# A two-layer encoder trunk on one core: one plain round of the first feed-forward matrix instead of two, the sums of x formed first, and the last step of the inverse variance moved back

## The chip, the core and the metric

The kernel runs on one core of a Trainium2 chip. The core has TensorE (PE in the profile, with its weight loads as PEld), VectorE (DVE), ScalarE (ACT), GpSimd (POOL), and SyncE (SP), whose queue issues most of the transfers. The metric is device time in microseconds (us) of one run: the median of three runs before is 1065.5 us (1065.3 to 1065.88).

## The reference

Two layers act on 512 rows of width 1024. The mixing part of a layer (three kinds of attention side by side) is not touched by the change. What is touched is the second half of each layer:

```
    x = x + jnp.concatenate([ya, yb, yc], axis=-1) @ w_out
    u = _rms(x, norm2) @ w_ff1
    return x + jnp.square(jax.nn.relu(u)) @ w_ff2
```

Here `_rms` divides a row by the root of its mean square (plus 1e-6) and multiplies it by the gain `norm2`. `w_ff1` is 1024 x 4096 and `w_ff2` is 4096 x 1024. Since relu followed by a square is homogeneous of degree two, the kernel leaves the division out of the first product and multiplies the result of the second by the inverse of the mean square.

## The kernel before

**Precision.** Every float32 matrix product is made of three: each operand is split into a rounded high part and a remainder (`whi`, `wlo` for weights, halves of `xhl` for x), and `mm3` (L262) issues high times high (L263), high times low (L264) and low times high (L265). The split of a weight block of 128x1024 (a "job") is one ScalarE copy (L205, writes `whi`) and one VectorE subtraction (L206, writes `wlo`). There are three buffers for each of `whi` and `wlo`, so a job's split can start once TensorE is done with the job three places earlier.

**The first feed-forward matrix** is worked through in 8 rounds (`NR`), each of 512 of its 4096 columns. The first `NSTD` = 2 rounds are plain: `ff1_std` (L1214) uses 4 jobs of 48 matmuls of 256 columns. The other six use Winograd's form of Strassen's product, which multiplies 2x2 blocks with 7 products instead of 8: `ff1_st` (L1245) uses 7 jobs of 24 matmuls, in the order `ORDER` (A11, S1, S2, A12, S4, S3, A22). S1 and S3 are sums of two blocks of weights that are added as the second is transferred (a second transfer with add, L160, on the GpSimd queue); S2 and S4 are formed by VectorE (L216, L220). A round of this kind also needs sums of blocks of x. `xsums` (L350) forms and splits them, a quarter at each of its 8 steps, in the buffer `xt`, and leaves them in `xbx`. The results of a round are rectified, squared, combined and split by `act`, `csplit`, `n1_`, `n2_`, `tail_` and `gsplit` (L1172 to L1206), mostly on VectorE.

**The second matrix** is worked through in 4 slices (`ff2`, L1306), each of which needs two rounds of the first. A slice has 14 products of 24 matmuls. `ff_pairs` (L117) interleaves one product of the second matrix with one of a Winograd round of the first, after the first `LEAD` = 0 products of the first matrix; both kinds of job stand in one list, and loads and splits run ahead in the order of that list.

**The inverse mean square.** `sqacc` (L322) sums the squares of x: 8 squares on ScalarE (into two halves of the buffer `ms`) and 7 additions on VectorE (L330, into `accs`). `emit_r2` (L1121) multiplies by a matrix of ones (L1123), negates (L1125), takes logarithm and exponential on ScalarE (L1128, L1129) and makes one Newton step on VectorE (L1130, L1131). Its first result (`nv`) is needed by the first `acc` (L1284) of the second matrix, its last (`r2`) only by the last slice. Before, this stood in the first plain round and `xsums` followed it.

**What sets the order.** The program is written as one stream; a scheduler then orders the instructions of each engine, and each engine takes them strictly in that order, waiting on semaphores. PSUM has 8 banks, which `bank()` hands out in turn. A product of `ff1_st` that starts from a copied bank (`Y`, L1248) adds onto it with matmuls that do not clear it.

Of the kernel before, what the change touches and what calls it, by code (L numbers as in the profile page):

```python
# [21 lines left out]
S = 512  # L22
# [22 lines left out]
NS = NR // 2  # L45
NSTD = 2
ORDER = ("A11", "S1", "S2", "A12", "S4", "S3", "A22")
# [3 lines left out]
def trunk(ctx, tc, x, cols, rows, gate_w, tabs, w_in, w_out, w1, w2, out):  # L51
# [43 lines left out]
    def v3(a, d=HD):  # L95
        return a.rearrange("p (h d) -> p h d", d=d)
# [3 lines left out]

    LEAD = 0
    RS_AT = 3
# [49 lines left out]
    free_raw, free_ff = deque(rawt), deque()  # L152
# [298 lines left out]
    for l in range(L):  # L451
# [663 lines left out]

        def bank():
            return banks.popleft()

        rr_ = {}

        def emit_r2():  # L1121
            pv = bank()
            T.matmul(pv, ones_m, sq_acc["t"], start=True, stop=True)  # L1123
            nv, lnv = ms_[:, :S], ms_[:, S:]
            V.tensor_scalar(nv, pv, -1.0, -EPS, ALU.mult, ALU.add)  # L1125
            banks.append(pv)
            r2 = cst.tile([P, S], F32, tag="aux", name=f"r2{l}")
            A.activation(lnv, nv, AF.Ln, scale=-1.0)  # L1128
            A.activation(r2, lnv, AF.Exp, scale=-1.0)  # L1129
            V.tensor_tensor(lnv, nv, r2, ALU.mult)  # L1130
            V.scalar_tensor_tensor(r2, lnv, 2.0, r2, ALU.add, ALU.mult)  # L1131
            rr_.update(nv=nv, r2=r2)

# [80 lines left out]
        def ff1_std(s, rr):  # L1214
            for i in range(2):
# [3 lines left out]
                for j in range(2):  # L1219
# [10 lines left out]
                    if j == 1:  # L1230
# [7 lines left out]
                        else:  # L1238
                            if rr:
                                units.extend(quads)  # L1240
# [4 lines left out]
        def ff1_st(s, rr):  # L1245
            X, Y = bank(), bank()
            prod1(X, 0)
# [58 lines left out]
        def ff2(s):  # L1306
# [37 lines left out]
            for dg in range(2):  # L1344
# [9 lines left out]
                give(s, dg, "t")  # L1354
                if s == 0 and dg:
                    free_ff.append(ms_)
                yield
# [3 lines left out]
        bg = None  # L1361
        for n_ in range(4 * NSTD):
            next(gens[1])
            if n_ == 0:
                for kx in range(KT):
                    sqacc(kx, kx == 0)
            if n_ == 3:
                emit_r2()
            if n_ == 1:
                xt_ = wt("xt", "xt")  # L1370
                bg = xsums(l, *(v3(xt_[:, i * S:(i + 1) * S], 256) for i in range(2)))
            if bg is not None:
                next(bg, None)
                next(bg, None)
        free_ff.append(xt_)
        for which, u in ff_pairs():
            next(gens[which])
        close_phase()
# [60 lines left out]
```

## Time and profile before

| | |
|---|---|
| median of the runs | 1065.5 us (1065.3 to 1065.88) |
| the profiled execution | 1065.74 us, of which the span of the profile is 1064.0 us |
| TensorE busy in the span | 1053.7 us (99%), 8768 matmuls |
| weight loads busy | 1002.8 us (94%) |
| VectorE busy | 904.2 us (85%) |
| ScalarE busy | 627.4 us (59%) |
| feed-forward part of layer 0 | first matmul at 222.78 us |
| feed-forward part of layer 1 | first matmul at 748.25 us |

How to read it: an engine's row gives its busy time, its share of the span and its instructions. Rows of a timeline give the start, the duration, the engine, the line, the operation with output and inputs, the shape, and in brackets how long the engine was idle before it and what it waited for. Instructions overlap at their ends: the pitch from one start to the next is what an instruction costs its engine. A matmul of 256 columns is shown as 0.28 us, but the next one starts 0.11 us later.

### The profile page before, as it was taken

Reading aid. Unit: us, or ns where it says so; the run is one execution under the profiler, and the core shown is the slowest. Engines: PE = TensorE matmul, PEld = TensorE weight load, DVE = VectorE, ACT = ScalarE, POOL = GpSimd, SP = SyncE. Lnnn points to the kernel's source line nnn. Section 1 sums busy time; section 2 is a strip of 40 time slices with the busy share of each in tenths; the row PEclk is TensorE's granted clock in tenths of the full one; section 3 lists DMA queues with packets and bytes.
Section 4 is the critical chain, followed back from the end, with each engine's and each line's share of the span. In section 5 each row is a group of like instructions: output and inputs, shape, how many; then the busy total and the mean of one; then the engine's idle time right before and its main releaser. Section 6 shows DMA issues by size and latency. Waiting matters only on the chain.

```text
span 1064.0 us, 21687 instructions
## 1 busy us (share of the span) xinstructions
PE 1053.7 (99%) x8768; PEld 1002.8 (94%) x8768; DVE 904.2 (85%) x1540; ACT 627.4 (59%) x1097; POOL 102.3 (10%) x154
## 2 busy tenths in 40 slices
PE   8999999999999999999999999999999999999998
PEld 8999977899999999999999998778999999999998
DVE  7696877899997988988977878688999888898797
ACT  6446655376666666567455467444766666666662
POOL 2030020100010000010002200101000101001000
PEclk9999999999999999999999999999999999999999
DMA  6523121165388687676135221213544886767752
GB/s 215 166 98 110 61 68 51 61 193 144 120 211 224 161 217 199 179 215 181 51 110 164 94 80 41 85 46 134 145 120 140 221 215 173 222 181 190 212 134 80
DMA packets 47365, 151.86 MB, mean 143 GB/s; under 512 B 5648, under 2 KB 8848, under 8 KB 47264
## 3 DMA queue, kind: packets, MB, share of 16 engines
q1 hardware_dynamic: 39056, 120.84, 34.0%
q0 software_dynamic: 8064, 29.36, 15.9%
q8 instruction: 69, 1.13, 0.4%
q14 instruction: 32, 0.26, 0.1%
q10 hardware_dynamic: 144, 0.26, 0.1%
HBM read 147.86 MB, written 2.13 MB: 141 GB/s over the span
## 4 chain that ended last, share of the span: by engine, by line
PE 85%; DVE 9%; ACT 3%; issue 1%; DMA 0%; SPq 0%; DVEq 0%
PE at L263 26%; PE at L265 26%; PE at L264 26%; DVE rt L726 2%; DVE wlo L206 2%; PE at L856 1%; PE at L898 1%; PE at L881 1%; ACT pe L769 1%; PE at L979 1%; DVE z L722 1%; DVE z L728 1%; PE at L756 1%; DMA raw<-in_w_in_dram 0%; DVE rb L407 0%
## 5 line engine op out<-in xcount | busy, mean ns | idle before, releaser
L205 ACT ACTIVATE whi<-raw 128x1024 fp32r<-128x1024 f32 (+1 forms) x130 | 136.2, 1048 | 114.6 <-PE at L264 87.8
L264 PE MATMUL at<-xhl,whi 128*128 128x256 f32 (+1 forms) x704 | 198.0, 281 | 0.0
L263 PE MATMUL at<-xhl,whi 128*128 128x256 f32 (+1 forms) x640 | 181.4, 283 | 0.0
L265 PE MATMUL at<-xhl,wlo 128*128 128x256 f32 (+1 forms) x640 | 180.4, 282 | 0.0
L263 PE MATMUL at<-yg,whi 128*128 128x256 f32 (+1 forms) x592 | 179.9, 307 | 0.5 <-DVE xT L1294 0.5
L206 DVE TENSOR_TENSOR wlo<-raw,whi 128x1024 fp32r<-128x1024 f32 (+1 forms) x130 | 157.4, 1211 | 27.0 <-ACT whi L205 26.6
L265 PE MATMUL at<-yg,wlo 128*128 128x256 f32 (+1 forms) x592 | 178.4, 301 | 0.0
L264 PE MATMUL at<-yg,whi 128*128 128x256 f32 (+1 forms) x560 | 169.4, 303 | 0.0
L263 PE MATMUL at<-whi,xhl 128*128 128x256 f32 (+1 forms) x576 | 163.0, 283 | 0.8 <-ACT xhl L334 0.7
L265 PE MATMUL at<-whi,xhl 128*128 128x256 f32 (+1 forms) x576 | 160.5, 279 | 0.6 <-DVE xhl L335 0.6
L264 PE MATMUL at<-wlo,xhl 128*128 128x256 f32 (+1 forms) x576 | 160.3, 278 | 0.5 <-DVE wlo L206 0.5
L205 ACT ACTIVATE whi<-fraw 128x1024 fp32r<-128x1024 f32 x100 | 106.1, 1061 | 83.9 <-PE at L264 79.6
L206 DVE TENSOR_TENSOR wlo<-fraw,whi 128x1024 fp32r<-128x1024 f32 x100 | 122.2, 1222 | 26.2 <-ACT whi L205 25.6
L264 PEld LDWEIGHTS at<-xhl,whi 128*128 128x128 f32 x704 | 132.2, 188 | 1.8 <-issue 0.5
L263 PEld LDWEIGHTS at<-xhl,whi 128*128 128x128 f32 x640 | 120.1, 188 | 1.7 <-ACT ct L1232 0.5
L265 PEld LDWEIGHTS at<-xhl,wlo 128*128 128x128 f32 x640 | 120.1, 188 | 1.2
L263 PEld LDWEIGHTS at<-yg,whi 128*128 128x128 f32 x592 | 111.2, 188 | 6.3 <-issue 1.7
L265 PEld LDWEIGHTS at<-yg,wlo 128*128 128x128 f32 x592 | 111.1, 188 | 5.3
L263 PEld LDWEIGHTS at<-whi,xhl 128*128 128x128 f32 x576 | 108.2, 188 | 1.8 <-ACT xhl L334 0.9
L264 PEld LDWEIGHTS at<-yg,whi 128*128 128x128 f32 x560 | 105.2, 188 | 4.2 <-DVE yg L1009 0.5
L265 PEld LDWEIGHTS at<-whi,xhl 128*128 128x128 f32 x576 | 108.2, 188 | 1.1 <-DVE xhl L335 1.0
L264 PEld LDWEIGHTS at<-wlo,xhl 128*128 128x128 f32 x576 | 108.4, 188 | 0.7 <-DVE wlo L206 0.7
(301 smaller groups left out, 2517.0 us busy)
## 6 DMA issues: line engine op xcount, KB each, us to landing
fraw<-in_w_dram SPq DMA_DIRECT2D x72, 512.0 KB, 4.9
raw<-in_w_dram SPq DMA_DIRECT2D x56, 512.0 KB, 4.3
raw<-in_w_in_dram SPq DMA_DIRECT2D x34, 512.0 KB, 3.5
fraw<-in_w_dram POOLq DMA_DIRECT2D x32, 512.0 KB, 6.3
raw<-in_w_out_dram SPq DMA_DIRECT2D x16, 512.0 KB, 3.2
xt<-in_w_dram SPq DMA_DIRECT2D x16, 512.0 KB, 5.1
raw<-in_w_dram POOLq DMA_DIRECT2D x14, 512.0 KB, 7.2
ms<-in_w_dram SPq DMA_DIRECT2D x12, 512.0 KB, 4.2
```

The source lines that it names most:

```text
L205: A.activation(hi[:, cs_], raw[:, cs_], AF.Copy)
L206: V.tensor_tensor(lo[:, cs_], raw[:, cs_], hi[:, cs_], ALU.subtract)
L263: T.matmul(o, sh, mh, start=first, stop=False, skip_group_check=skip)
L264: T.matmul(o, sh, ml, start=False, stop=False, skip_group_check=skip)
L265: T.matmul(o, sl, mh, start=False, stop=last, skip_group_check=skip)
L722: V.tensor_tensor(z10, z10, bc(rq), ALU.mult)
L726: V.tensor_tensor(r10[:, oo:oo + n, a:a + 32], z10[:, oo:oo + n, b:b + 32], tb(S_, n, a, a + 32), ALU.mult)
L728: V.tensor_tensor(zaq[t], ro[:, :640], rt[:, :640], ALU.add)
L756: T.matmul(sc[r][:, g * 256:g * 256 + nk], qTA[g][r * 64:(r + 1) * 64, c * P:(c + 1) * P], kTA[r * 64:(r + 1) * 64, k0:k0 + nk], start=Tru ...
L769: A.activation(pe[:, u, :nk], sc[u % 2][:, (u // 2) * 256:(u // 2) * 256 + nk], AF.Exp, bias=nmx[:, u:u + 1], accum_out=ssum[:, u:u + 1])
L856: T.matmul(sp[:, :nk], qTB[rs, pr, n * P:(n + 1) * P], kTB[rs, pr, :nk], start=True, stop=False)
L881: T.transpose(pt[:, b * P:(b + 1) * P], scs[r][:, b * P:(b + 1) * P], ident)
```

## The change

`NSTD` becomes 1: round 1 of the first matrix is now a Winograd round. `LEAD` becomes 7: the 7 products of that round come before the first product of the second matrix, and from there on the interleaving is the same as before. `xsums` is now run by the first four steps (two quarters after each plain product), ahead of `sqacc`, which follows after the fifth; `emit_r2` follows after the eighth, and its last two VectorE instructions become `finish_r2`, which is called at the end of the first slice of the second matrix. The buffer `xt` goes back to the ring of load buffers after the fifth step. `bank()` remembers which banks have been used, and `Y` is now taken from those. Lines from L1116 on have other numbers in the changed kernel: L1123, L1125, L1130 and L1131 become L1128, L1130, L1139 and L1140; L1184, L1196, L1199, L1200, L1205, L1264, L1270 and L1293 become those numbers plus 8.

```
-NSTD = 2
+NSTD = 1
...
-    LEAD = 0
+    LEAD = 7
...
-        def bank():
-            return banks.popleft()
+        full = set()
+
+        def bank(seeded=False):
+            b = next(b for b in banks if not seeded or id(b) in full)
+            banks.remove(b)
+            full.add(id(b))
+            return b
...
             A.activation(r2, lnv, AF.Exp, scale=-1.0)
+            rr_.update(nv=nv, lnv=lnv, r2=r2)
+
+        def finish_r2():
+            nv, lnv, r2 = (rr_[n] for n in ("nv", "lnv", "r2"))
             V.tensor_tensor(lnv, nv, r2, ALU.mult)
             V.scalar_tensor_tensor(r2, lnv, 2.0, r2, ALU.add, ALU.mult)
-            rr_.update(nv=nv, r2=r2)
...
-                            if rr:
+                            if rr == NSTD - 1:
                                 units.extend(quads)
...
-            X, Y = bank(), bank()
+            X, Y = bank(), bank(True)
...
                 if s == 0 and dg:
+                    finish_r2()
                     free_ff.append(ms_)
...
-        for n_ in range(4 * NSTD):
-            next(gens[1])
+        for n_, (which, u) in enumerate([(1, None)] * 4 * NSTD + list(ff_pairs())):
+            next(gens[which])
             if n_ == 0:
+                xt_ = wt("xt", "xt")
+                bg = xsums(l, *(v3(xt_[:, i * S:(i + 1) * S], 256) for i in range(2)))
+            if n_ < 4:
+                next(bg)
+                next(bg)
+            if n_ == 4:
                 for kx in range(KT):
                     sqacc(kx, kx == 0)
-            if n_ == 3:
+                free_ff.append(xt_)
+            if n_ == 7:
                 emit_r2()
-            if n_ == 1:
-                xt_ = wt("xt", "xt")
-                bg = xsums(l, *(v3(xt_[:, i * S:(i + 1) * S], 256) for i in range(2)))
-            if bg is not None:
-                next(bg, None)
-                next(bg, None)
-        free_ff.append(xt_)
-        for which, u in ff_pairs():
-            next(gens[which])
```

What this does to the order is shown at three places of layer 0 (layer 1 has the same rows). The first is VectorE just after the start of the feed-forward part, from the split of the third plain job on. Before:

```order
L206 TENSOR_TENSOR wlo_2975<-raw_75,whi_2974 128x1024
L330 TENSOR_TENSOR accs_3027<-accs_3027,ms_2865 128x512
L364 SCALAR_TENSOR_TENSOR xt_3103<-xT,pcol,xt_3103 128x256
L330 TENSOR_TENSOR accs_3027<-accs_3027,ms_2865 128x512
L364 SCALAR_TENSOR_TENSOR xt_3103<-xT,pcol,xt_3103 128x256
L330 TENSOR_TENSOR accs_3027<-accs_3027,ms_2865 128x512
L206 TENSOR_TENSOR wlo_3044<-fraw_2869,whi_3043 128x1024
```

The same place now:

```order
L206 TENSOR_TENSOR wlo_2976<-fraw_2868,whi_2975 128x1024
L364 SCALAR_TENSOR_TENSOR xt_3029<-xT,pcol,xt_3029 128x256 x2
L368 SCALAR_TENSOR_TENSOR xt_3029<-xT,pcol,xt_3029 128x256 x2
L330 TENSOR_TENSOR accs_3273<-accs_3273,ms_2864 128x512
L206 TENSOR_TENSOR wlo_3041<-fraw_2868,whi_3040 128x1024
L358 TENSOR_TENSOR xbx_2865<-xt_3029,xbx_2865 128x512 x2
```

The sums of x (L364, L368, L358) have moved ahead of most of the sums of squares (L330), which are now spread over what follows.

The second place is VectorE at the end of what stands ahead of the second matrix. Before, `wlo_3320` is the last plain job and `wlo_3379` the first job of the second matrix:

```order
L1184 TENSOR_TENSOR gx_2867<-ct_2868,gx_2867 128x1024 x2
L1130 TENSOR_TENSOR ms_2865<-ms_2865,r_3237 128x512
L1205 SCALAR_TENSOR_TENSOR ct_2868<-ct_2868 128x512
L1131 SCALAR_TENSOR_TENSOR r_3237<-ms_2865,r_3237 128x512
L375 SCALAR_TENSOR_TENSOR xt_3103<-xT,pcol,xt_3103 128x256 x2
L1184 TENSOR_TENSOR yg<-ct_2868,gx_2867 128x1024
L356 SCALAR_TENSOR_TENSOR xbx_2866<-xt_3103,xbx_2866 128x512
L206 TENSOR_TENSOR wlo_3320<-raw_73,whi_3319 128x1024
L1293 SCALAR_TENSOR_TENSOR xT<-xT,ms_2865 128x2x256 x2
L206 TENSOR_TENSOR wlo_3379<-raw_75,whi_3378 128x1024
```

Now the same splits of round 0 (L1192) are followed by jobs of the new Winograd round, S2 (`wlo_3238`), A12 (`wlo_3291`), S4 (`wlo_3321`) and S3 (`wlo_3353`):

```order
L206 TENSOR_TENSOR wlo_3238<-fraw_2868,whi_3237 128x1024
L1207 SCALAR_TENSOR_TENSOR ct_2867<-ct_2867 128x512
L1208 TENSOR_TENSOR ct_2867<-ct_2867 128x512
L356 SCALAR_TENSOR_TENSOR xbx_2865<-xt_3029,xbx_2865 128x512
L1192 TENSOR_TENSOR gx_2866<-ct_2867,gx_2866 128x1024 x2
L1213 SCALAR_TENSOR_TENSOR ct_2867<-ct_2867 128x512
L206 TENSOR_TENSOR wlo_3291<-raw_73,whi_3290 128x1024
L220 TENSOR_TENSOR fraw_2868<-raw_73,fraw_2868 128x1024
L1192 TENSOR_TENSOR yg<-ct_2867,gx_2866 128x1024
L1130 TENSOR_SCALAR ms_2864<-at_2972 128x512
L206 TENSOR_TENSOR wlo_3321<-fraw_2868,whi_3320 128x1024
L206 TENSOR_TENSOR wlo_3353<-raw_75,whi_3352 128x1024
```

Between the splits of S2 and A12 stand six other instructions, and the two instructions of the Newton step are gone from here.

The third place is TensorE around the product with the matrix of ones. Before, it stands between the first and the second plain round:

```order
L265 MATMUL at_2968<-xhl,wlo_3044 128x256
L1123 MATMUL at_2969<-accs_3027,ones_m 128x512
L263 MATMUL at_2970<-xhl,whi_3114 128x256
L264 MATMUL at_2970<-xhl,whi_3114 128x256
L265 MATMUL at_2970<-xhl,wlo_3115 128x256
```

Now it stands inside the product A12, right ahead of the first matmul that uses the low part of A12's job:

```order
L265 MATMUL at_2970<-xbx_2865,wlo_3238 128x256
L263 MATMUL at_2966<-xhl,whi_3290 128x256
L264 MATMUL at_2966<-xhl,whi_3290 128x256
L1128 MATMUL at_2972<-accs_3273,ones_m 128x512
L265 MATMUL at_2966<-xhl,wlo_3291 128x256
```

The product of ones now follows round 0, the three products A11, S1 and S2 and two matmuls of A12. (L1128 is the changed kernel's number; before, L1128 is the logarithm on ScalarE.) At the end of the Winograd round the first product of the second matrix is begun ahead of A22, the round's last; thirteen of its matmuls come first, then the 24 of A22, then the other eleven:

```order
L265 MATMUL at_2970<-xbx_2865,wlo_3353 128x256
L263 MATMUL at_2973<-gx_2866,whi_3424 128x256
L264 MATMUL at_2973<-gx_2866,whi_3424 128x256
L265 MATMUL at_2973<-gx_2866,wlo_3425 128x256
```

Before, the first product of the second matrix (`whi_3378`) followed the last matmul of the second plain round. Now its job (`whi_3424`, `wlo_3425`) is asked for 24 matmuls earlier in the row than the order of the products says.

## The prediction

> **What bounds the kernel now.** I read the page first, then the stretch of each layer that the change rewrites, then single instructions there. The page, its engines and one group:
>
> ```profile
> PE 1053.7 (99%) x8768; PEld 1002.8 (94%) x8768; DVE 904.2 (85%) x1540; ACT 627.4 (59%) x1097; POOL 102.3 (10%) x154
> L206 DVE TENSOR_TENSOR wlo<-fraw,whi 128x1024 fp32r<-128x1024 f32 x100 | 122.2, 1222 | 26.2 <-ACT whi L205 25.6
> ```
>
> TensorE is the bound over the span. But 85% is an average, so the next view is busy time by stage. The first two stages run, in layers 0 and 1, from the first matmul of the feed-forward part to the first product of the second matrix, which is what the change rewrites; the others follow in layer 0. The columns are length, then PE, PEld, DVE, ACT and POOL busy, granted clock, DMA share and rate.
>
> ```profile
> 222.78:266.96 44.18, 44.18 (x387) 43.70 (x386) 44.01 (x67) 29.50 (x44) 3.60 (x4) 1.00 0.54 132
> 748.25:792.43 44.18, 44.18 (x387) 43.70 (x386) 44.01 (x67) 29.49 (x43) 3.49 (x4) 1.00 0.54 132
> 260.00:280.00 20.00, 20.00 (x179) 20.00 (x178) 19.40 (x24) 11.79 (x14) 0.81 (x1) 1.00 0.44 120
> 280.00:300.00 20.00, 20.00 (x179) 20.00 (x178) 18.13 (x19) 11.26 (x15) 0.86 (x1) 1.00 0.51 150
> 300.00:350.00 50.00, 50.00 (x443) 50.00 (x442) 42.85 (x46) 33.72 (x41) 6.04 (x7) 1.00 0.81 206
> ```
>
> In the rewritten stretch VectorE is as full as TensorE: 44.01 of 44.18 us, the same in both layers. It has air again only after 280 us. The clock is 1.00 throughout. What VectorE's queue looks like there (start, duration):
>
> ```profile
> 226.40 1.22 DVE L206 TENSOR_TENSOR wlo<-raw,whi 128x1024 fp32r<-128x1024 f32 x1
> 227.53 0.68 DVE L330 TENSOR_TENSOR accs<-accs,ms 128x512 f32<-128x512 f32 x1
> 228.13 0.48 DVE L364 SCALAR_TENSOR_TENSOR xt<-xT,pcol,xt 128x256 f32<-128x256 f32 x1
> 228.53 0.68 DVE L330 TENSOR_TENSOR accs<-accs,ms 128x512 f32<-128x512 f32 x1
> ...
> 258.44 1.22 DVE L206 TENSOR_TENSOR wlo<-raw,whi 128x1024 fp32r<-128x1024 f32 x1
> ```
>
> The pitches, start to start, are 1.14 us for an instruction of 1024 elements, 0.60 for 512 and 0.40 for 256. The last row is the split for the first product of the second matrix, over at about 259.58. TensorE there:
>
> ```profile
> 222.78 0.37 PE L263 MATMUL at<-xhl,whi 128*128 128x256 f32 x1
> ...
> 244.53 0.28 PE L265 MATMUL at<-xhl,wlo 128*128 128x256 f32 x1
> 244.64 1.02 PE L1123 MATMUL at<-accs,ones_m 128*128 128x512 f32 x2
> ...
> 267.27 0.28 PE L263 MATMUL at<-gx,whi 128*128 128x256 f32 x1
> ...
> 269.99 0.28 PE L263 MATMUL at<-xhl,whi 128*128 128x256 f32 x1
> ```
>
> ```profile
> 244.80 0.86 PE at L1123 x2
> ```
>
> From 267.27 to 269.99 lie the 24 matmuls of one product: 2.72 us, 0.1134 each. The product of ones costs 0.86 on the chain. Round 0 is over at 244.64. That product needs its low part with its third matmul, 0.23 after 267.27, at 267.50, so before the change VectorE is 7.9 us ahead at this point.
>
> **The change part by part.** Less on TensorE: a plain round has 4 x 48 = 192 matmuls, a Winograd round 7 x 24 = 168. 24 x 0.1134 = 2.72 us per layer, 5.44 in both. This is the whole gain.
>
> More on VectorE: counting the rows of the order from the split at 226.40 up to and with the split of the second matrix's first job, there were 10 of 1024 elements, 25 of 512 and 16 of 256; now there are 15, 25 and 16. The five are three more job splits (11 for 8) and the sums S2 and S4. Two of 512 left with the Newton step and others came with the Winograd round. With unrounded pitches (1.137, 0.602, 0.397) the sum was 32.77 us, and the trace has 33.18 (226.40 to 259.58), so the waits inside were 0.41. Now it is 38.46: 5.69 more. At the same time TensorE asks earlier: 2.72 for the missing matmuls, and another 2.72 because this job now stands ahead of A22 in its queue. 7.9 - 5.69 - 5.44 = -3.2: what was 7.9 us early is 3.2 us late, and TensorE waits for it.
>
> The same sum at each job of the new round, now with the waits between the engines. They need ScalarE's pitches:
>
> ```profile
> 244.49 0.58 ACT L1232 ACTIVATE ct<-at 128x512 f32<-128x512 f32 x1
> 244.96 1.05 ACT L205 ACTIVATE whi<-fraw 128x1024 fp32r<-128x1024 f32 x1
> 245.91 0.59 ACT L1232 ACTIVATE ct<-at 128x512 f32<-128x512 f32 x1
> 246.39 0.63 ACT L354 ACTIVATE xbx<-xt 128x512 fp32r<-128x512 f32 x1
> 246.91 1.06 ACT L1234 ACTIVATE ct<-ct 128x1024 f32<-128x1024 f32 x1
> ```
>
> So 0.95 for 1024 elements, about 0.5 for 512. Without waits TensorE would begin A11 at 244.64, S1 at 247.36, S2 at 250.08 and A12 at 252.80. VectorE's rows give the low part of S2 at 250.0, in time to a tenth. Behind it stand the recombination of round 0 and its three splits, and A12's low part comes only after 9, 20 and 16 rows, 28.62 us: 255.0 by the sum, 255.8 with the waits (the second split of round 0 waits for a ScalarE that is behind its own queue of squares, copies and `whi`, until 252.2). TensorE has two matmuls and the product of ones to do meanwhile (0.23 + 0.86, to 253.9) and then stands: 2.06 us. S4's low part follows two instructions of 1024 and others later, at 259.9, where TensorE, resumed, is at 258.9: 1.05. The first product of the second matrix: low part at 265.7, TensorE at 265.2: 0.6. Together 3.7 us; by the sums alone, with no wait between engines, the latest is 2.9. I take 3.7, since the waits are in the order, and add 0.2 of the weight load that a wait leaves uncovered (the bound is one of 188 ns at each of three stops). Behind each stop stands the whole rest of the phase: TensorE takes its matmuls in order, and ScalarE's next `whi` need a buffer that TensorE frees. The weight load's row:
>
> ```profile
> L264 PEld LDWEIGHTS at<-xhl,whi 128*128 128x128 f32 x704 | 132.2, 188 | 1.8 <-issue 0.5
> ```
>
> After that the two engines run level. TensorE needs 5.44 us for a pair of products; VectorE's pair is about 4.9 as long as the xT rows of the first slice are scaled. Up to the second product of round 3 I count 44, 51 and 16 rows, 87.08 us, so 313.5, or 314.5 with the waits so far, and TensorE, 3.7 late, asks at 314.7. It just holds; there is nothing to spare, and any idle time of VectorE above some tenths before 315 us would lengthen the wait.
>
> Net per layer: 3.7 + 0.2 - 2.72 = 1.2 us slower; two layers, 2.4. Against the profiled execution: span 1064.0 + 2.4 = 1066.4, plus the 1.74 around it, 1068.1; the median run was 0.24 shorter than it. **Forecast 1067.9 us.** The bounds: 2.9 of wait and nothing uncovered give +0.2 per layer, 1065.9; 5 us of wait (1.3 more of idle VectorE, which now idles 1.87 in the stage from 280 to 300) give +2.5 per layer, 1070.5.
>
> At nothing I cost these: *The Newton step* (`finish_r2`), moved to the end of the first slice.
>
> ```profile
> L1130 DVE TENSOR_TENSOR ms<-ms,r x2: 685/685/685, 251.8 to 777.1; 128x512 f32<-128x512 f32 x2
> L1131 DVE SCALAR_TENSOR_TENSOR r<-ms,r x2: 690/690/690, 253.0 to 778.3; 128x512 f32<-128x512 f32 x2
> ```
>
> Its result is used only in the last slice; it takes 1.2 us out of the full stretch, which the counts contain. *The bank rule* makes Y a bank of round 0, evacuated some 15 us before. *Transfers*: a Winograd round loads 7 blocks for 4 and adds two on the GpSimd queue.
>
> ```profile
> fraw<-in_w_dram SPq DMA_DIRECT2D x72, 512.0 KB, 4.9
> fraw<-in_w_dram POOLq DMA_DIRECT2D x32, 512.0 KB, 6.3
> ```
>
> ```profile
> 211.80 1.75 SPq L158 DMA_DIRECT2D fraw<-in_w_dram  x4
> ```
>
> S1's two take 11.2 in series and are asked for with the first blocks at 211.80; they land near 225 and by my count are first read after 239. `xt` comes back to the ring some 20 us earlier, which helps the later ones. If this cover went, each us of a late block would be a us.
>
> **A rule against the sum.** The granted clock is 1.00 in every stage quoted. The Trainium skill, "TensorE: Matmul & The Clock Gate" (Part 1: The HAM clock gate), says that an idle window of about 3.4 us brings the clock down to half until a busy window has passed. No stop in my sum is that long, and no run here shows such a stop yet; it is a rival below, priced by itself.
>
> **The rivals.** *A, the gain comes through.* If VectorE's extra work fits ahead of need, TensorE stays the bound and the time is 1065.5 - 5.4 = 1060.1. For it: 99% busy TensorE, and stretches where VectorE idles only for ScalarE's `whi`, which itself waits for TensorE. Against it: 44.01 of 44.18, and five long instructions more in less time. The Trainium skill, "Perfetto Trace Analysis" (Identifying the Most-Contended Engine), would judge TensorE by the share of its weight loads, which is 94% here; by that rule alone this rival would be the forecast. 10%.
>
> *B, the two sides cancel.* The waits between engines hide in one another and only the sums count: 2.9 lost, 2.72 gained, 1065.9; or VectorE makes up a little of it. For it: in the stretch before, the trace's waits were only 0.41. Against it: A12's split follows three splits that need ScalarE's results first. 33%.
>
> *C, ScalarE ends last.* It gets three more `whi` (0.95 each) and about 1.9 us of evictions in 41.5 us, on 29.5 busy: 34 of 41.5. A12's `whi` stands behind two splits that wait for VectorE; my count has it at 253.2, 1.5 us before VectorE wants it. If it slips by 3 us, 1.5 us a layer come on top: 1070.9. 10%.
>
> *D, the clock falls* at the stop at A12: the 22 matmuls up to the next stop (2.5 us) take twice as long, of which 1.05 would have been the stop at S4: 1.45 per layer, 1067.9 + 2.9 = 1070.8. By the page's window it would be 3.4 us at half the pace, 1.7 per layer, 1071.3. For it only that the stops of a layer lie within 15 us; against it, two matmuls and the product of ones stand in the middle of the longest. 4%.
>
> **How the numbers follow.** Forecast 43%, A 10%, B 33%, C 10%, D 4%. About 0.2% (2.1 us) is what a measurement can tell from no change: 1063.4 to 1067.6. The forecast's own range is 1066 to 1070.5 and a quarter of it lies below 1067.6. Slower: three quarters of 43, C, D, and 3 of B, 49%; faster: A and a little of B, 13%; the rest, 38%, within. The range that leaves no more than two in ten out: 1064.3 to 1071.2.
>
> **What would show it.** Right: in the changed profile TensorE stops in both layers for `wlo` (VectorE L206) inside A12 for about 2 us, again at S4 and at the first product of the second matrix; VectorE has no idle time over half a us from 226 to 266; the product of ones starts in the first of these stops; after A22 TensorE is at about 271.0, where it now is at 269.99 with the same products done. Wrong: if TensorE shows no stops there (A), if the stops end on ScalarE (C) or on a transfer, if the clock column falls (D), or if VectorE's pitches differ from those here.

## The result and the profile after

Of 22 runs of the changed kernel none took about the 1067.9 us that was forecast. Eleven lie between 1065.78 and 1066.94 us (median 1066.15), ten between 1076.23 and 1077.04 (median 1076.6), and one at 1087.13; the median of all, 1071.59, is the middle of a gap and is 0.4 above the upper end of the range. The kernel before, run beside it 22 times, stays between 1064.87 and 1066.3, median 1065.74. The ratio of the means is 1.0051, 95% interval 1.0034 to 1.0068; it leaves out the one run at 1087. The groups are 10.5 us apart, so two things need an answer: what the change costs in the lowest group (0.4 us, 0.2 per layer), and what adds 10.5 us once or twice.

The profiled execution is one of the second group (1076.6 us, span 1074.9), so its trace holds both cases. Two lines of its page, and its stages with the columns of the stage table in the prediction; the third and fifth stage are 50 us from the middle of the feed-forward part of layer 0 and of layer 1:

```profile
PE 1060.3 (99%) x8720; PEld 1007.8 (94%) x8720; DVE 916.2 (85%) x1554; ACT 635.6 (59%) x1113; POOL 105.8 (10%) x158
...
PEclk9999999999999999999999999999999999999999
```

```profile
222.78:266.96 44.18, 42.08 (x357) 40.75 (x357) 44.08 (x65) 33.80 (x51) 2.58 (x3) 1.00 0.53 145
266.96:320.00 53.04, 53.04 (x470) 53.04 (x470) 53.01 (x61) 35.42 (x43) 4.32 (x5) 1.00 0.65 177
350.00:400.00 50.00, 50.00 (x444) 50.00 (x443) 44.97 (x47) 31.41 (x38) 4.33 (x5) 1.00 0.73 197
748.20:792.00 43.80, 41.81 (x353) 40.46 (x352) 43.70 (x65) 33.42 (x50) 2.58 (x3) 1.00 0.55 148
850.00:900.00 50.00, 50.00 (x426) 50.00 (x426) 41.22 (x44) 30.62 (x37) 5.21 (x6) 1.00 0.73 193
```

In the rewritten stretch VectorE is busy for 44.08 of 44.18 us, and TensorE, which was full, is 2.10 us short and does 357 matmuls where it did 387. What TensorE waits for between 222 and 270 us (in total, times, longest), and the places (VectorE's low parts first, then TensorE):

```profile
PE at L265 <- DVE wlo L206: 1.5, 2, 1.2
PE at L263 <- ACT ct L1264: 0.6, 1, 0.6
```

```profile
253.86 1.22 DVE L206 TENSOR_TENSOR wlo<-raw,whi 128x1024 fp32r<-128x1024 f32 x1
...
257.87 1.22 DVE L206 TENSOR_TENSOR wlo<-fraw,whi 128x1024 fp32r<-128x1024 f32 x1
...
263.69 1.22 DVE L206 TENSOR_TENSOR wlo<-fraw,whi 128x1024 fp32r<-128x1024 f32 x1
```

```profile
252.80 0.28 PE L264 MATMUL at<-xhl,whi 128*128 128x256 f32 x1
252.91 1.02 PE L1128 MATMUL at<-accs,ones_m 128*128 128x512 f32 x2
255.14 0.39 PE L265 MATMUL at<-xhl,wlo 128*128 128x256 f32 x1 [1.20 <-DVE wlo L206]
255.36 0.28 PE L263 MATMUL at<-xhl,whi 128*128 128x256 f32 x1
...
258.80 0.39 PE L263 MATMUL at<-xbx,whi 128*128 128x256 f32 x1 [0.56 <-ACT ct L1264]
259.02 0.28 PE L264 MATMUL at<-xbx,whi 128*128 128x256 f32 x1
259.14 0.39 PE L265 MATMUL at<-xhl,wlo 128*128 128x256 f32 x1
...
264.97 0.39 PE L265 MATMUL at<-gx,wlo 128*128 128x256 f32 x1 [0.33 <-DVE wlo L206]
```

The stops stand where they were forecast: at A12, behind the product of ones; at S4, with S3's first two matmuls among it; and at the first product of the second matrix. From start to start, less the pitch, they are 1.37 us (255.14 less 252.91 and 0.86), 0.73 and 0.49, 2.6 in all.

Each of them ends with a low part of VectorE. With VectorE's pitch of 1.14 the three low parts are ready at 255.00, 259.00 and 264.83, and the matmuls that need them start 0.14 later each time, at 255.14, 259.14 and 264.97. That holds for the second stop too, whose wait the first view puts down to ScalarE's copy (L1264): the copy held up only the two matmuls of S3, which had to be over by 259.14 and were.

Two smaller costs come on top. At five places (252.80, 255.36, 259.02, 259.36 and 265.19) a matmul follows the one before it after 0.22 us instead of 0.11, which adds 0.5. And the 24 matmuls between the first two stops go at the slower spacing described below, which adds 0.1. With the 2.72 gained, the stretch should lose 0.5 us, and it does. Its two ends:

```profile
222.53 0.37 PE L263 MATMUL at<-xhl,whi 128*128 128x256 f32 x1
...
270.30 0.28 PE L263 MATMUL at<-xhl,whi 128*128 128x256 f32 x1
```

The first product of round 2, A11, starts 47.77 us behind the layer's first matmul, where it was 47.21 (269.99 less 222.78): 0.56 us lost. Part of it is made up later, outside the rewritten stretch: from the first feed-forward matmul of layer 0 to that of layer 1 (748.08) there are 525.55 us, where there were 525.36 (to 748.14). So layer 0, which is at the faster spacing in this trace, loses 0.2 us, as the lowest group has it.

The other 10.5 us are in the third and the fifth stage. In both TensorE has no idle time and the clock is 1.00, yet it does 444 matmuls in 50 us of layer 0 and 426 in 50 us of layer 1. The kernel before did 444 in both; its layer 1:

```profile
850.00:900.00 50.00, 50.00 (x444) 50.00 (x443) 44.15 (x48) 32.29 (x39) 4.35 (x5) 1.00 0.75 193
```

One group of matmuls of the changed kernel from each stage, by shape:

```profile
L263 PE MATMUL at<-xbx,whi 128*128 128x256 f32 x48 | 13.2, 276 | 0.0
...
L263 PE MATMUL at<-xhl,whi 128*128 128x256 f32 x58 | 16.3, 281 | 0.0
```

Taken as differences of consecutive start times in the trace, the spacing is 113.3 ns in layer 0 and 117.8 in layer 1. Layer 1 has the slower spacing from its first stop at 778 us to a stop at 1069, a dozen matmuls before its end. From the last stop of the rewritten stretch, at 790.6, that is some 2,370 matmuls x 4.45 ns = 10.5 us: the step between the groups. Counting steps in the times of all the runs, 12 of 44 layers had it.

### The profile page after: what moved, and what is told of

Same layout as the page of the kernel before. It is cut to its first block, busy times and chain, and to the rows that moved or that the text cites. A ratio compares the mean times of both kernels' runs of the same rounds, so it can differ in the third digit from the quotient of the medians.

```text
span 1074.9 us, 21637 instructions
## 1 busy us (share of the span) xinstructions
PE 1060.3 (99%) x8720; PEld 1007.8 (94%) x8720; DVE 916.2 (85%) x1554; ACT 635.6 (59%) x1113; POOL 105.8 (10%) x158
## 4 chain that ended last, share of the span: by engine, by line
PE 76%; DVE 18%; ACT 3%; issue 2%; DMA 0%; SPq 0%; DVEq 0%
PE at L263 23%; PE at L265 23%; PE at L264 23%; DVE wlo L206 4%; DVE rt L726 2%; DVE xhl L335 1%; PE at L856 1%; PE at L898 1%; DVE accs L330 1%; PE at L881 1%; ACT pe L769 1%; DVE xT L587 1%; PE at L979 1%; DVE z L728 1%; DVE z L722 1%
## 5 line engine op out<-in xcount | busy, mean ns | idle before, releaser
L205 ACT ACTIVATE whi<-raw 128x1024 fp32r<-128x1024 f32 (+1 forms) x136 | 142.4, 1047 | 114.1 <-PE at L264 83.7
L206 DVE TENSOR_TENSOR wlo<-raw,whi 128x1024 fp32r<-128x1024 f32 (+1 forms) x136 | 164.1, 1207 | 26.7 <-ACT whi L205 26.3
L264 PE MATMUL at<-xhl,whi 128*128 128x256 f32 (+1 forms) x624 | 177.1, 284 | 0.0
L265 PE MATMUL at<-xhl,wlo 128*128 128x256 f32 (+1 forms) x560 | 159.8, 285 | 2.4 <-DVE wlo L206 2.4
L263 PE MATMUL at<-xhl,whi 128*128 128x256 f32 (+1 forms) x560 | 159.7, 285 | 0.0
L263 PE MATMUL at<-xbx,whi 128*128 128x256 f32 x448 | 124.9, 279 | 1.1 <-ACT ct L1264 1.1
L264 PE MATMUL at<-xbx,whi 128*128 128x256 f32 x448 | 124.7, 278 | 0.0
L265 PE MATMUL at<-xbx,wlo 128*128 128x256 f32 x448 | 124.7, 278 | 0.0
L264 PEld LDWEIGHTS at<-xhl,whi 128*128 128x128 f32 x624 | 117.2, 188 | 1.3
L265 PEld LDWEIGHTS at<-xhl,wlo 128*128 128x128 f32 x560 | 105.9, 189 | 5.4 <-DVE wlo L206 4.1
L263 PEld LDWEIGHTS at<-whi,xhl 128*128 128x128 f32 x576 | 108.3, 188 | 2.2 <-ACT whi L205 1.1
```

The costliest lines, as they stand in the source:

```text
L205: A.activation(hi[:, cs_], raw[:, cs_], AF.Copy)
L206: V.tensor_tensor(lo[:, cs_], raw[:, cs_], hi[:, cs_], ALU.subtract)
L263: T.matmul(o, sh, mh, start=first, stop=False, skip_group_check=skip)
L264: T.matmul(o, sh, ml, start=False, stop=False, skip_group_check=skip)
L265: T.matmul(o, sl, mh, start=False, stop=last, skip_group_check=skip)
```

## The experiments

Where a kernel's runs lie in steps of some 10.5 us, the lowest group is compared with the lowest of the changed kernel, 1066.15, and the steps are counted as layers with the slower spacing. Only one run of each kernel has a trace, so for the others this is an inference from the time.

**1. The additions of the squares on GpSimd.**

```
-            V.tensor_tensor(sq_acc["t"], sq_acc["t"], sq, ALU.add)
+            (G if "sq" in phase else V).tensor_tensor(sq_acc["t"], sq_acc["t"], sq, ALU.add)
```

> The changed kernel, but the seven additions of the squares of x (L330) run on GpSimd instead of VectorE. That takes 7 x 0.602 = 4.2 us out of VectorE's queue ahead of A12; on GpSimd the nearest row is 1.46 us for one 128x512 tensor operation, 10.2 us in all, which fits between the first square at about 229 and the product of ones at about 253. Theory 1 (VectorE is late, and a TensorE stop for a late weight decides in which of two matmul paces, about 113 or about 118 ns, the stream goes on until the next stop): A12's low part is ready at about 249.7 instead of 253.9, ahead of the 253.0 at which TensorE asks, the stops at A12, S3 and the first product of the second matrix go, the gain of 2.72 us per layer comes through, and every run is at 1060 to 1061, none 10 us above it. Theory 2 (the order or the placement of the products itself, not the stops, brings the slower pace): the lowest runs are at 1060 to 1061 too, but others lie 10.5 or 21 us above them, in the same share as in the changed kernel. Theory 3 (VectorE is not what TensorE waits for; ScalarE is): the lowest runs stay at 1066.

Measured: 1073.05 to 1073.88 in four runs, 1083.1 and 1083.4 in two. The first row below is what TensorE waits for from 222 to 270 us, the others are stages around that stop:

```profile
PE at L263 <- ACT at L1256: 4.0, 1, 4.0
```

```profile
250.00:253.90 3.90, 0.00 (x0) 0.00 (x0) 3.90 (x6) 3.90 (x7) 0.76 (x1) 1.00 0.62 98
253.96:257.60 3.64, 3.64 (x18) 3.64 (x19) 3.64 (x5) 3.23 (x4) 0.00 (x0) 0.53 0.73 217
257.60:261.00 3.40, 3.40 (x31) 3.40 (x31) 3.40 (x4) 2.19 (x3) 0.86 (x1) 1.00 0.32 120
```

All three theories failed. GpSimd was too slow for its place: ScalarE's squares have two buffers, so ScalarE waited for GpSimd's additions (4.0 us by the trace, over three squares), VectorE's instructions beside them were stretched (a split took 2.31 us instead of 1.22), the sums of x came late, and S2 stopped for 4.2 us on ScalarE's copy of a bank. Behind that stop the granted clock is 0.53 for 3.6 us; layer 1 stops as long, and its clock is 0.50 from 783.5 to 786.7. That is rival D of the prediction, at a stop longer than any in the changed kernel (1.4 us, clock 1.00). The Trainium skill, "TensorE: Matmul & The Clock Gate" (Part 1: The HAM clock gate), names a window of about 3.4 us, idle or busy, for each switch; the trace agrees.

**2. A late VectorE in the old kernel.** Every plain job's low part is written twice. (The second added line is cut at its start.)

```
-            V.tensor_tensor(lo[:, cs_], raw[:, cs_], hi[:, cs_], ALU.subtract)
+            [V.tensor_tensor(lo[:, cs_], raw[:, cs_], hi[:, cs_], ALU.subtract) for _ in range(jb.get("times", 1))]
...
+            jobs.append(...); [j.update(times=2) for j in jobs if j["ff"] == l and j["which"] is None]
```

> The kernel before, with each low part of the eight plain jobs of the feed-forward part written twice by VectorE (the same result): 8 x 1.14 = 9.1 us more in VectorE's queue, against a lead of 7.9 us at the first product of the second matrix. Nothing else of the change is in it. Theory 1: VectorE is 1 to 2 us late there, TensorE stops, the lowest runs are at 1067.5 to 1070, and some runs lie 10.5 or 21 us above the lowest, since the stop alone is enough to start the slower pace. Theory 2: one group of runs at 1067.5 to 1070, with matmuls 113 ns apart in both layers, since the order of the products is the old one.

Measured: 1071.03 to 1071.54 in four runs and 1092.16 in the fifth, which is the profiled one: both layers have the slower spacing there (427 matmuls in 50 us). With the old order of products and nothing of the change, late low parts are enough to bring it, though in one run of five. The lowest runs lie 1.0 to 1.5 above the expected range: TensorE waited 1.6 us for a low part and 0.3 for ScalarE, by the waits of that trace, where 1.2 was the plain sum.

**3. The new order in the old kernel**, with two plain rounds (`NSTD` = 2, `LEAD` = 0; `xsums`, `sqacc`, `emit_r2` and `finish_r2` as in the changed kernel).

> The kernel before, still with two plain rounds, but with the other two parts of the change: the sums of x first, the squares behind them, the product of ones behind the eighth plain step, and the last step of the inverse variance at the end of the first slice. VectorE's sum ahead of the first product of the second matrix changes by little, and 1.2 us of it are moved out. Both theories on the waits expect no stop longer than the product of ones itself and 1065.2 to 1066.2, one group of runs. If the slower pace came from this new order (a variant of theory 2), some runs would lie 10.5 or 21 us above.

Measured: 1074.96 to 1077.89, all four. What TensorE waits for from 222 to 310 us, and a row of VectorE's timeline ahead of it:

```profile
PE at L263 <- DVE ct L1273: 0.8, 1, 0.8
```

```profile
296.57 1.22 DVE L220 TENSOR_TENSOR fraw<-fraw 128x1024 f32<-128x1024 f32 x1 [1.05 <-DMA fraw<-in_w_dram]
```

All four lie 9 to 12 us above the lowest group, as the variant of theory 2 has it, but the slower spacing follows a stop that no theory expected: VectorE waits 1.05 us for a transfer at 296, the evacuation of a bank is late at 303, and from that stop on layer 0 runs at the slower spacing (426 matmuls in 50 us; layer 1, with a stop of 1.6 us at 840, at 443). A likely reason for the late transfer is a load buffer. The buffer `ms` takes a block again, before and in this run, at:

```profile
267.91 0.33 SPq L158 DMA_DIRECT2D ms<-in_w_dram  x1
...
316.99 0.33 SPq L158 DMA_DIRECT2D ms<-in_w_dram  x1
```

Its contents are now read until 316 us, so the loads do without this buffer for 49 us more. That it made this transfer late was not tested. The changed kernel gets `ms` back as late (314.69), and neither TensorE, VectorE nor ScalarE waited for a transfer there; the prediction counted only `xt`, which comes back earlier. None of the four runs was faster than the kernel before.

**4. One more split on VectorE** ahead of A12 in the changed kernel (as in 2, for S2 of the first Winograd round alone).

> The changed kernel with the low part of S2 of the first Winograd round written twice by VectorE (the same result): 1.14 us more in its queue per layer, ahead of A12. Theory 1: VectorE sets this stretch, so each us of it is a us of the layer: the lowest runs are at 1066.2 + 2 x 1.1 = 1068.5, and others 10.5 and 21 us above. If waits on ScalarE or on transfers set it (theory 3), the extra 1.14 us hide and the lowest runs stay at 1066 to 1066.6.

Measured: 1068.49 to 1068.8 in four runs, 1070.41 in one, whose feed-forward part already starts over 1 us later. A us of VectorE in the lead-in (the rewritten stretch) is a us of the layer, 2.4 for 2.3. None of these ten layers kept the slower spacing, though they stop as often; at the changed kernel's 12 of 44 that would happen by chance about four times in a hundred (an estimate, 32/44 to the tenth power).

**5. The sums S2 and S4 on GpSimd.**

```
-            V.tensor_tensor(a, g["S1"]["raw"], a, ALU.add)
+            (G if jb.get("pool") else V).tensor_tensor(a, g["S1"]["raw"], a, ALU.add)
...
```

> The changed kernel, with the two sums of weight blocks of the first Winograd round (S2 and S4, L216 and L220, 1.14 us each on VectorE) formed by GpSimd, whose work nothing on ScalarE waits for until whi of the same job. By the GpSimd row of 1.46 us for 512 elements they take about 2.9 us each there. Theory 1 (VectorE's queue sets the lead-in): A12's low part starts at 252.7 instead of 253.9 and ends as TensorE asks; S4's, S3's and the first one of the second matrix come 2.3 us earlier; of the 2.55 us of stops per layer a few tenths are left, and the lowest runs are at 1061 to 1062. If a stop of some tenths is left, runs 10.5 us above may remain; if none is, they go. Theory 3 (ScalarE sets it, as it did in the first experiment): the lowest runs stay above 1065.

Measured: 1084.31 to 1094.77. The first sum on GpSimd, and VectorE beside it:

```profile
237.58 3.98 POOL L216 TENSOR_TENSOR fraw<-fraw 128x1024 f32<-128x1024 f32 x1 [5.59 <-DVE wlo L206]
```

```profile
238.61 0.68 DVE L1197 TENSOR_TENSOR gx<-ct,gx 128x512 fp32r<-128x512 f32 x1
239.21 3.02 DVE L364 SCALAR_TENSOR_TENSOR xt<-xT,pcol,xt 128x256 f32<-128x256 f32 x2
242.16 0.87 DVE L368 SCALAR_TENSOR_TENSOR xt<-xT,pcol,xt 128x256 f32<-128x256 f32 x2
```

The two instructions of L364 take 3.02 together, where they take 0.87 in the changed kernel. The first of them has 2.63 of it and ends 0.28 behind GpSimd's addition. Beside the second sum an instruction of L1208 takes 2.90 instead of 0.69. The work moved to GpSimd was paid by VectorE in waiting, about 2.2 us for an addition that costs it 1.14, so theory 1 failed: A12's low part starts at 257.0 and not at the expected 252.7. The Trainium skill, "SBUF — State Buffer" (SBUF: two separate sides), says that the two engines share a pair of ports as an exclusive lock, against a VectorE instruction with two SBUF inputs among others; the trace agrees in that beside each of the two additions one such instruction is held until GpSimd is done. In this run, too, TensorE stops for about 3.5 us at A12 in both layers. Behind the one the clock stays at 1.00, behind the other it falls:

```profile
258.40:261.00 2.60, 2.60 (x22) 2.60 (x23) 2.60 (x3) 1.42 (x2) 0.00 (x0) 1.00 0.60 198
796.10:799.20 3.10, 3.10 (x15) 3.10 (x16) 3.10 (x4) 1.44 (x2) 0.00 (x0) 0.50 0.61 192
```

The slower spacing begins in it at 306 us, where TensorE stops for no time that the profile lists as a wait. The matmuls there, and the mean of one in the stretches from 280 to 305 and from 307 to 330:

```profile
305.93 0.28 PE L265 MATMUL at<-yg,wlo 128*128 128x256 f32 x1
306.05 0.36 PE L263 MATMUL at<-xbx,whi 128*128 128x256 f32 x1
306.24 0.28 PE L264 MATMUL at<-xbx,whi 128*128 128x256 f32 x1
```

```profile
L265 PE MATMUL at<-xbx,wlo 128*128 128x256 f32 x22 | 6.1, 276 | 0.0
...
L265 PE MATMUL at<-xbx,wlo 128*128 128x256 f32 x22 | 6.2, 281 | 0.0
```

The stream slips by less than 0.1 us (0.12 and 0.19 between starts instead of twice 0.11), and is slower from there on.

**6. A small product behind the last stop** of the changed kernel, its result unused.

```
+            if n_ == 12:
+                T.matmul(banks[-1][:, :P], ones_m, ones_m, start=True, stop=True)
```

> The changed kernel with one product of a 128x128 float32 constant with itself (L1386, as L1226 does at the start of the part) per layer, about 10 us behind the last stop, its result unused. Theory 1a (the pace of the stream is set anew by anything that breaks it, and such a float32 product sets it to 113 ns; in the first experiment layer 1 went at 117 before the product of ones and at 113 behind it): one group of runs, at 1066.2 + 2 x 0.25 = 1066.7, none 10 us above. Theory 1b (only a stop sets the pace, and it outlives other instructions): about three runs in ten layers stay slow, so groups at 1066.7 and 1077.

Measured: 1076.96 to 1077.16 three times, 1086.47 to 1087.67 three times, 9 layers of 12. In the trace both layers are at 113.3 ns ahead of the product and at 117.8 behind it. Layer 1 from 803 to 809 and from 811 to 817 us:

```profile
L263 PE MATMUL at<-xbx,whi 128*128 128x256 f32 x8 | 2.2, 276 | 0.0
...
L263 PE MATMUL at<-xbx,whi 128*128 128x256 f32 x8 | 2.2, 281 | 0.0
```

Both theories failed in their detail: it need not be a stop, but this product does not restore the faster spacing, it takes it away.

**7. The Newton step back in its old place.**

```
+            V.tensor_tensor(lnv, nv, r2, ALU.mult)
+            V.scalar_tensor_tensor(r2, lnv, 2.0, r2, ALU.add, ALU.mult)
...
-                    finish_r2()
```

> The changed kernel without its third part: the two instructions of the last step of the inverse variance (L1139 and L1140, 0.60 us each on VectorE) stand right behind the exponential again. Theory 1: they stand ahead of the split of the first product of the second matrix in VectorE's queue, each us is a us, and the lowest runs are at 1066.2 + 2 x 1.2 = 1068.6, or 1067.4 where one of the two slips behind that split. If the stop at that product ends on something else, 1066.2.

Measured: 1067.37 to 1067.85 in the lowest four of twelve runs, six at 1077.3 to 1078.4, two at 1087.3 and 1088.0. The lowest are near the smaller of the two expected values: moving the step out of the lead-in is worth 0.6 to 0.9 us per layer, (1067.37 - 1066.15) / 2 to (1067.85 - 1066.15) / 2.

**8. The squares first**, as before the change (`sqacc` at `n_ == 0` ahead of `xsums`).

> The changed kernel without its second part: the squares of x are formed ahead of the sums of x again, as before. VectorE has the same instructions ahead of A12, only in another order. Theory 1 with the plain sum of the queue: A12's low part comes at the same time, the sums are ready by the time S1 and S2 ask (247.4 and 250.1), and the lowest runs stay at 1066.2, within 0.5. If the sums' chain between ScalarE and VectorE is what the order was for, S1 or S2 waits for xbx, 1 to 4 us per layer more: 1068 to 1074.

Measured: 1066.38 to 1067.72 in eight runs, 1076.7 to 1077.5 in four. TensorE from 222 to 270 us:

```profile
PE at L263 <- ACT ct L1264: 0.9, 1, 0.9
PE at L265 <- DVE wlo L206: 0.3, 1, 0.3
PE at L263 <- ACT at L1256: 0.3, 1, 0.3
```

A new wait at S2 and a shorter one for low parts: the order moves the waits and is worth about 0.3 us per layer (1066.73, the median of the eight, less 1066.15, in two layers). The sum of VectorE's queue, which is the same in both, counts for more than its order.

**9. The squares summed on TensorE.**

```
+    ones_r = cst.tile([P, P], F32R, name="ones_r")
+    A.activation(ones_r, ones_m, AF.Copy)
...
+    def sqprod(k, pv):
+        sq = yg[:, 12 + k % 4]
+        A.activation(sq, xT[:, k], AF.Square)
+        T.matmul(pv, ones_r, sq, start=k == 0, stop=k == KT - 1)
...
-            T.matmul(pv, ones_m, sq_acc["t"], start=True, stop=True)
...
-                    sqacc(kx, kx == 0)
+                    sqprod(kx, pv_)
```

> The changed kernel, with the mean square of x formed another way: ScalarE writes the eight squares as one-pass float32r (rounded to that format; nothing else of the computation differs), TensorE sums them with eight products of 512 columns, and VectorE's seven additions (4.2 us per layer) and the two-pass product of ones (0.86 us) go. Eight such products cost about 8 x 0.227 = 1.8 us, by the 226 to 227 ns between 512-column products ahead of the part, so TensorE has 0.95 us more to do. No work goes to GpSimd. Theory 1 (VectorE's queue sets the lead-in): the 2.55 us of stops per layer go, and the lowest runs are at 1066.2 - 2 x (2.55 - 0.95) = 1063.0, between 1062 and 1064. Theory 3 (ScalarE sets it): 1066 and above. Whether runs 10.5 us above remain depends on whether a break of the stream, these products among them, is followed by the slower pace: if only stops start it, none remain; if products of another shape do too, some remain.

Measured: 1063.81 to 1064.77 in all eleven runs, median 1064.54, against 1065.52 of the kernel before on the same chip: 0.9989 (0.9981 to 0.9998). Half of the expected gain came, as TensorE waits for ScalarE's fifth square and later for an evacuation:

```profile
PE at L338 <- ACT yg L337: 0.5, 1, 0.5
PE at L263 <- DVE ct L1285: 0.3, 1, 0.3
```

It is faster than the kernel before, by 1.0 us. No layer of 22 kept the slower spacing, though eight products and two stops break TensorE's stream: layer 1 of the trace falls into it at 778 us and leaves it at the break at 790.

**10. A full float32 product of 512 columns** at the place of the small one in 6.

> The changed kernel with one more two-pass float32 product of 512 columns per layer (L1386, ones by a block of x, result unused) at the place where the 128-column one of an earlier run stood, about 10 us behind the last stop. That one was followed by 118 ns in both layers; the product of ones, which has this shape, was followed by 113 ns in every trace read so far. If the shape of what breaks the stream decides the pace: one group of runs at 1066.2 + 2 x 0.75 = 1067.7, none 10 us above. If any break is a draw: groups at 1067.7, 1078 and 1089.

Measured: 1078.71 once, 1088.26 to 1089.04 five times: 11 layers of 12. Here, too, the trace has 113.3 ns ahead of it and 117.8 behind it, in both layers. The shape of the product does not decide. The premise did not hold in the changed kernel's own trace either: behind the product of ones and the stop that follows it, from 255.36 to 257.95, the matmuls are 117.6 ns apart.

**11. Eight places for the squares** (`yg[:, 8 + k]` in 9).

> The kernel with the squares summed on TensorE, with eight places for the squares instead of four, so that ScalarE writes all of them before 235 us and the eight products stand in one piece behind S1. In the run with four places TensorE waited 0.5 to 0.6 us per layer for the fifth square (ScalarE, L337) and then took the last four one by one among the matmuls of S2. Theory 1: that wait goes and nothing replaces it before the first product of the second matrix: 1064.55 - 2 x 0.5 to 0.7 = 1063.1 to 1063.6, one group. If the wait only moves to the next late operand (VectorE's low parts), 1064 to 1064.6.

Measured: 1084.86 to 1085.49, all four, both layers at the slower spacing in the trace. Less 21 us for that, it would be at 1064.0, an estimate, where the second of the two expectations has it. The wait for the square is gone, and two for VectorE stand in its place:

```profile
PE at L263 <- DVE ct L1285: 0.4, 1, 0.4
PE at L265 <- DVE wlo L206: 0.3, 1, 0.3
```

**12. The squares on TensorE in the old kernel**, with two plain rounds.

> The kernel before, with two plain rounds and nothing of the change, and the same eight products of squares in place of VectorE's seven additions and the product of ones (8 x 0.231 - 0.86 = 0.98 us more on TensorE per layer, 4.2 us less on VectorE). Theory 1 (before the change TensorE sets the stretch, VectorE being 7.9 us ahead at the first product of the second matrix): the relief of VectorE is worth nothing there and the products cost their time, 1065.5 + 2 x 0.98 = 1067.5. If VectorE or ScalarE had held TensorE back in the old kernel too, it would be at 1065 or below.

Measured: 1067.0 to 1068.11, median 1067.65, ratio 1.0018 (1.0009 to 1.0027). That is 0.93 us per layer above the 1065.8 of the kernel before on the same chip, close to the 0.98 that the products cost, and TensorE waits for nothing between 222 and 270 us in its trace. The kernel before is bound by TensorE in this stretch. Against experiment 9 the plain round is worth (1067.65 - 1064.54) / 2 = 1.55 us per layer once VectorE is relieved, of 2.72, or 1.4 if each is taken against the kernel before on its own chip; the two differ in the order and in the places of the squares as well. With VectorE as it was, the plain round is worth nothing.

## Why the prediction was right and wrong

**The bound** was read rightly: 44.01 of 44.18 us in a stage of TensorE and VectorE alike, and five long instructions more in VectorE's queue. The stretch became VectorE's. Experiments 4, 7 and 9 show it from both sides: 1.14 us more cost 1.2, the Newton step's 1.2 cost 0.6 to 0.9, and 4.2 less brought 0.8 in spite of 0.98 more on TensorE. No stop of the changed kernel's lead-in ended on a transfer, which were costed at nothing.

**The gain** of 24 matmuls, 2.72 us, was taken out and given back in waits, at the three places named, all three for the low parts named.

**The size of the waits** was the term that was mis-sized: 3.7 us forecast, 2.6 measured (2.06 and 1.37 at A12, 1.05 and 0.73 at S4, 0.6 and 0.49 at the second matrix). The failed step is the 0.8 us of waits between the engines that was added to the sums. Counted from the split with which the sums begin (226.40 before, 226.20 now), A12's low part is ready after 28.80 us, where the sum alone was 28.62, and that of the second matrix after 38.63, where it was 38.46. So 0.2 of the 0.8 was there: when VectorE's turn came, ScalarE's results were ready but for 0.1 us of idle time in 44.18. The matmuls behind the stops cost 0.5 instead of the 0.2 put down for uncovered weight loads. So a layer lost 0.2 us and not 1.2, and the lowest group, 1066.15, is where rival B put it (1065.9) and for its reason. The sign that was to be seen at 271.0 stands at 270.30.

**After 266 us** VectorE "just holds": 53.01 of 53.04 us busy until 320, and TensorE without a gap. This was right, with nothing to spare.

**Rivals** C and D did not happen in the changed kernel: ScalarE's one late evacuation lay within a wait for VectorE, and the clock stayed at 1.00. A had its cause right (the gain exists) and its condition wrong.

**What was missing** is the spacing. The prediction took 0.1134 us per matmul for the whole of the feed-forward part. It said that "behind each stop stands the whole rest of the phase" and counted that rest at an unchanged pitch. A stop of 0.5 us can be followed by 10.5 us more, and this, not the waits, sets where the median lies. The trace of before already had the other spacing, at two places that the prediction left out: behind a stop at 1058.51 the last dozen matmuls of layer 1 are 118 ns apart, and so are those of the next layer's first products from 534 to 546 us. The stop, and one group of those products (first before, from 535 to 545 us, then in the changed kernel, from 536 to 545):

```profile
1058.51 0.39 PE L263 MATMUL at<-yg,whi 128*128 128x256 f32 x1 [0.51 <-DVE xT L1294]
```

```profile
L263 PE MATMUL at<-whi,xhl 128*128 128x256 f32 x29 | 8.1, 281 | 0.0
...
L263 PE MATMUL at<-whi,xhl 128*128 128x256 f32 x28 | 7.7, 276 | 0.0
```

Where these products begin, at 534, the kernel before goes over from 113 to 118 ns, and the changed kernel from 118 to 113.

**Luck.** The direction was forecast, by a mechanism that cost 0.4 us in both layers and not 2.4. That the middle of all the runs comes near the end of the range of 1064.3 to 1071.2 (the median 1071.6 above it, 1.0051 x 1065.5 = 1070.9 within it) is luck: it lies between two groups, with no run near it, and comes from a cause that the prediction did not have. With one run more in the lowest group and one less in the next the median would have been inside the lowest group.

**Not settled** is what decides between the two spacings. It is not the granted clock, not an engine that is waited for, not the new order of products (experiment 2 has it without), not the length of the stop alone (0.1 us is enough in 5, and the stops of 4 all end well), and not the shape of what breaks the stream (6 and 10). Nor is it the chip alone: 9 and 10 ran on one chip, 11 and 12 on another, with opposite outcomes, and the kernel before stayed between 1064.87 and 1066.46 in its 88 runs beside them all. Each kernel has its own odds, from 0 of 22 layers (9, 12) and 12 of 44 (the changed kernel) to 11 of 12 (10) and 8 of 8 (11). That the changed kernel and 4, which stop at the same places, differ in it may be chance.

## What to carry to other kernels

Where two engines are both full in a stage, take the sum of the second one's queue by its pitches before taking work off the first; here that sum was good to 0.2 us in 38, and waits between the engines added on top of it made the forecast worse. A change that trades a few matmuls for a stop should be timed in many runs and judged by their groups, since one profile or a median of few shows only one side. Work moved off a full VectorE belongs on an engine that does not hold it up; in this kernel that was TensorE, and not GpSimd.

## What the runs showed of the hardware that was not expected

- A stream of weight loads and matmuls of 256 columns runs at 113.3 or at 117.8 ns from start to start, at the same granted clock of 1.00, and keeps to one of them for thousands of matmuls. A break of the stream, even one of less than 0.1 us or another product in it, can be followed by the other, in either direction. It can also change where the products of one matrix end and those of the next begin, with no stop to be seen (at 534 us). The kernel before has the slower one too, for short stretches (from 534 to 546 us, and the last dozen matmuls).
- An addition of 128x1024 elements on GpSimd held up VectorE for about 2.2 us (experiment 5), more than the 1.14 it costs on VectorE itself.
- A TensorE stop of 4.2 us was followed by a granted clock of 0.53 and 0.50 for some 3.5 us in both layers of experiment 1; one of 3.5 us did so in one of two layers of experiment 5, and no stop of up to 1.8 us in the feed-forward parts of the traces did.
